# A two-layer decoder trunk: the mLSTM group's projections folded into score and gate weights, loras by differences, two longer pauses

## The chip, the core and the metric

The kernel runs on one core of a Trainium2 chip. The metric is the device time of one execution in microseconds (us). Each core has a matrix engine (TensorE, "PE" in the profile; its weight loads are "PEld"), a vector engine (VectorE, "DVE"), a scalar engine (ScalarE, "ACT"), a small general engine (GpSimd, "POOL"), and SyncE ("SP"), whose in-order queue issues all the DMA transfers of this kernel.

## The reference, cut to what matters

There are 256 tokens of 2048 features, in float32, and two layers. Layer 0 makes `u = h @ w_in`, and its columns feed two groups that run side by side. One is an RG-LRU. The other is an mLSTM group, which the change touches:

```python
xmc = silu(causal_dwconv(xm, m_conv_w, m_conv_b))
q = block_diag(xmc, m_wq)          # 512 blocks of 4x4
k = block_diag(xmc, m_wk)
v = block_diag(xm, m_wv)
qkv = concatenate([q, k, v])
ig = qkv @ m_wi + m_bi             # 8 heads
fg = qkv @ m_wf + m_bf
ym = mlstm_chunkwise(q, k, v, ig, fg)   # needs the scores q @ k^T
```

Layer 1 is RWKV-7 time mixing. Two low-rank branches ("loras") take shifted inputs:

```python
dh = shift_right(h) - h
xw = h + dh * mu_w;  xa = h + dh * mu_a
w_log = ... tanh(xw @ w1) @ w2 ...
a     = sigmoid(a0 + (xa @ a1) @ a2)
```

and the delta rule is computed in chunks of 64 tokens, for which triangular 64x64 matrices are inverted, 32x32 blocks first, which are then merged.

## The kernel before

All large products run on TensorE with each weight split in two parts (`whi`, made by ScalarE, and `wlo`, the rest, made by VectorE), and the activations likewise (`hh`, `hl`). A weight piece is 128x1024 (512 KB). `load_w` fetches it through SP's queue into one of four `raw` buffers, `split_w` makes the two parts (three buffers each), and `in_mms` issues the matmuls into the banks `gb`. An input projection (`in_proj`) takes 8 such pieces of 24 matmuls and gives 512 columns of `u`.

All work around these products is written as Python generators. Each runs in a lane of a small planner (`Weave`). A generator issues some instructions and then yields a number, its pause, in units of the planner's clock; `in_mms` moves that clock on by 0.44 after every few matmuls (`wv_.tick`), 2.64 per piece. When a pause is over, the next section of the generator is issued between the matmuls. `wv_.drain(gen)` runs a generator to its end at once. TensorE's order is exactly this order of issue (`InOrder`). The other engines' queues are ordered by a scheduler, in which the splits of the weights go ahead of other work; each queue is then executed in order.

The parts that the change touches:

- `mlstm_in(c, xm)`, for the quarters c = 0 to 3 of the mLSTM group (512 features, two heads each). It runs the convolution, forms `xm2` = 2 silu(conv), spreads the 4x4 blocks into block-diagonal 128x128 weights `we` (VectorE), multiplies (q and k on TensorE, copied to `qk`; v in token order, copied to `vtok`), sums up the gates' pre-activations (from `wif`, q, k, and `gv`, the v projection folded into the gate weights) and the scores `S`. The generator of quarter c is still under way when the next input projection ends, and is drained there, so its TensorE part lies in one block between two projections.
- `tables()` loads and prepares constants during the first projection; `gates()` turns the gates' sums into the row `Mt` per head; `head(hd)` spreads that row over 128 partitions by a matmul with `sel`.
- `loras()` in layer 1: 8 pieces of 128x384. Per piece VectorE makes `wb` from the loaded lora weights `raw` and the vectors mu (three products, three differences), then follows the split, and 18 matmuls. The three banks' parts `q0`, `q1`, `q2` give `hid`.
- `decay(g, st)` for the groups g = 0 to 7 of layer 1: it loads the second lora weight `l2` (named `l` in the profile) and multiplies it with `hid`. From its results come `Pe`, then `keys` makes `AR` and `BK`, and `blocks` needs these.
- `inverse(g, st)`: VectorE inverts the 32x32 blocks; two rounds of small matmuls then merge them. The first round is `mb<-ZT,Aab`; ScalarE copies the result into `ZT`; the second is `mb<-TT,ZT`. Between the two stands a pause (`yield 2.6`).

Most matmuls are issued at L117, and the instructions of VectorE and ScalarE at L133, the helpers' lines; groups are therefore told apart by their tiles.

Of the kernel before, what the change touches and what calls it, by code (L numbers as in the profile page):

```python
# [144 lines left out]
def two_layers(ctx, tc, x, gpost, cst, selc, v0, v1, w_in0, w_out0, w_in1, w_out1, lruw, qkvw,  # L145
# [274 lines left out]
    with ExitStack() as l0:  # L420
# [36 lines left out]
        wiff = c0.tile([P, 2048], F32, name="wif", tag="wg")[:, 0:1920].rearrange("p (a b) -> p a b", a=48)  # L457
        qkvs = c0.tile([P, 4, 16, 4], F32, name="qkvs")
        sel = c0.tile([8, 8, P], F32, name="sel")
# [40 lines left out]

        def mlstm_in(c, xm):
            xc = t4("xc")
            for f in range(4):
                i = 4 * c + f
                conv(xc[:, f, :], xm[:, f, :], [vs0(f"mw{j}", i) for j in range(4)], vs0("mb", i))
                yield 6.76
# [5 lines left out]
            we = [t4("we") for _ in range(2)]  # L512
            wv = [w.rearrange("p a t -> p (a t)").rearrange("p (w f o) -> p w f o", w=2, f=4) for w in we]
            for m in range(4):
                for f in range(4):
                    dve.tensor_tensor(
                        wv[m // 2][:, m % 2, f, :].rearrange("p (b o) -> p b o", o=4),
                        qkvs[:, m, 4 * c + f, :].unsqueeze(1).broadcast_to([P, 32, 4]),
                        blk.unsqueeze(2).broadcast_to([P, 32, 4]), MUL)
                yield 4.0 if m == 3 else 1.0  # L520
            wq, wk, wvv, wvT = (wv[m // 2][:, m % 2] for m in range(4))
            qk = [t4("qk") for _ in range(2)]
            for f in range(4):
                b = mbank()
                pe.matmul(b[:, 0:T], lhsT=wq[:, f, :], rhs=xm2[:, f, :], start=True, stop=True, skip_group_check=True)
                pe.matmul(b[:, T:2 * T], lhsT=wk[:, f, :], rhs=xm2[:, f, :], start=False, stop=True, skip_group_check=True)
                activ(qk[f // 2][:, 2 * (f % 2):2 * (f % 2) + 2, :], b.rearrange("p (a t) -> p a t", a=2), AF.Copy, scale=0.5)
                yield 0.6
            qt = lambda f: qk[f // 2][:, 2 * (f % 2), :]
            kt = lambda f: qk[f // 2][:, 2 * (f % 2) + 1, :]  # L530
# [7 lines left out]
            gv = s0.tile([P, 160], F32, name="gv", tag="gv", bufs=1)  # L538
            b = mbank()
            for f in range(4):  # L540
                pe.matmul(b[:, f * 40:(f + 1) * 40], lhsT=wvT[:, f, :], rhs=wiff[:, 32 + 4 * c + f, :],
                          start=(f == 0), stop=True, skip_group_check=True)
            dve.tensor_copy(gv, b[:, 0:160])
            yield 0.96

            ops = []
            for f in range(4):
                i = 4 * c + f
                ops += [(wiff[:, i, :], qt(f)), (wiff[:, 16 + i, :], kt(f)), (gv[:, f * 40:(f + 1) * 40], xm[:, f, :])]
            b = mbank()  # L550
            for n, (w, r) in enumerate(ops):
                o = b[64 * (n % 2):64 * (n % 2) + 40, 0:T]
                pe.matmul(o, lhsT=w, rhs=r, start=(n < 2), stop=(n >= 10), skip_group_check=True)
                if n % 4 == 3:
                    yield 0.5
# [6 lines left out]
            for hd in range(2):  # L562
                b = mbank()
                for j, (lo_, w_) in enumerate(((0, T), (P, P))):
                    o = b[:, 0:T] if j == 0 else b[:, T:T + P]
                    for f in range(2):
                        pe.matmul(o, lhsT=kt(2 * hd + f)[:, j * P:(j + 1) * P], rhs=qt(2 * hd + f)[:, lo_:T],
                                  start=(j == 0 and f == 0), stop=(f == 1), skip_group_check=True)
                activ(S[:, 2 * c + hd, :], b[:, 0:384], AF.Copy, scale=0.0625)
                yield 0.8  # L570

        gt = c0.tile([8, 8, T], F32, name="gt", tag="wg")
        gf, gi, e, r1, r2, r3, aj, Mt = (gt[:, i, :] for i in range(8))
# [168 lines left out]
    with ExitStack() as l1:  # L742
# [39 lines left out]
        def loras():  # L782

            banks = [gbank(), gbank()]
            for pc in range(8):
                raw = wp.tile([P, 2, 512], F32, name="raw", tag="raw", bufs=RAW_BUFS)
                nc.sync.dma_start(raw[:, :, 0:192], lora1[pc].rearrange("p (k f) -> p k f", k=2))
                wb = t4("wb", (2, 384))
                for wc, oc, n, nm in ((0, 128, 96, "muw"), (160, 224, 32, "mua"), (96, 320, 64, "mua")):
                    ac = {128: 0, 224: 96, 320: 256}[oc]  # L790
# [10 lines left out]
            act.copy(sh[0:64, 0, :], q2[64:128])
            act.copy(sh[64:96, 0, :], q1[96:128])
            dve.tensor_tensor(hid[:, 1, 1:T], hid[:, 1, 1:T], sh[:, 0, 0:T - 1], ADD)
            activ(hid[:, 0, :], hid[:, 0, :], AF.Tanh)
# [145 lines left out]
        def inverse(g, st):  # L950
# [47 lines left out]
            yield 2.6  # L998
# [313 lines left out]
```

## Time and profile before

| | |
|---|---|
| runs | 1907.44, 1913.1 and 1910.84 us, median 1910.84 |
| profiled execution | 1908.97 us, its span 1907.2 us, granted TensorE clock 0.993 |
| TensorE busy | 1877.9 us (98%) |
| VectorE, ScalarE, GpSimd busy | 1394.5 us (73%), 1057.2 us (55%), 63.3 us (3%) |
| DMA | 299.63 MB, 157 GB/s on average |

Layer 0's projections and heads lie in the first 470 us of the span, its output projection ends about 640 us, and layer 1 fills the rest. In the rows of the timeline the first number is the start in us from the span's start, the second how long the row's group lasts, then come engine, line, operation, output tile <- input tiles, rows*columns of the array that a matmul uses, its output's shape, and how many. "mb" and "gb" are banks of the results' memory. A float32 matmul of the program is two instructions in the trace; a split one is one. A time in square brackets is idle time of the engine before the row, and what ended it. Since matmuls are pipelined, the distance between two starts tells what one costs in a stream, not its own duration.

### The profile page before, as it was taken

Reading aid. Unit: us, or ns where it says so; the run is one execution under the profiler, and the core shown is the slowest. Engines: PE = TensorE matmul, PEld = TensorE weight load, DVE = VectorE, ACT = ScalarE, POOL = GpSimd, SP = SyncE. Lnnn points to the kernel's source line nnn. Section 1 sums busy time; section 2 is a strip of 40 time slices with the busy share of each in tenths; the row PEclk is TensorE's granted clock in tenths of the full one; section 3 lists DMA queues with packets and bytes.
Section 4 is the critical chain, followed back from the end, with each engine's and each line's share of the span. In section 5 each row is a group of like instructions: output and inputs, shape, how many; then the busy total and the mean of one; then the engine's idle time right before and its main releaser. Section 6 shows DMA issues by size and latency. Waiting matters only on the chain.

```text
span 1907.2 us, 39575 instructions
## 1 busy us (share of the span) xinstructions
PE 1877.9 (98%) x16507; PEld 1738.9 (91%) x16507; DVE 1394.5 (73%) x2302; ACT 1057.2 (55%) x1633; POOL 63.3 (3%) x92
## 2 busy tenths in 40 slices
PE   9999999999999999999999999999999999999998
PEld 8999999999888899989999999999999999997886
DVE  5667777766554669979689689597697896895544
ACT  5444666644444546565565656655655655665442
POOL 0000000000000000000010010000100100100000
PEclk9999999999999999999999999999999999999999
DMA  7433545445655543434434334344344333356654
GB/s 250 143 133 111 175 159 176 150 171 187 225 201 203 176 144 131 154 120 145 145 131 144 123 131 156 117 147 145 109 155 138 138 134 133 123 183 210 213 199 158
DMA packets 86947, 299.63 MB, mean 157 GB/s; under 512 B 9576, under 2 KB 12392, under 8 KB 86768
## 3 DMA queue, kind: packets, MB, share of 16 engines
q1 hardware_dynamic: 86768, 297.11, 45.0%
q8 instruction: 129, 2.11, 0.4%
q14 instruction: 50, 0.41, 0.1%
HBM read 289.20 MB, written 7.86 MB: 156 GB/s over the span
## 4 chain that ended last, share of the span: by engine, by line
PE 90%; DVE 5%; ACT 2%; issue 1%; DMA 1%; POOL 0%; DVEq 0%; SPq 0%; POOLq 0%; ACTq 0%
PE gb L117 73%; PE mb L117 16%; DVE wlo L133 2%; PE mb L120 2%; ACT whi L133 1%; DVE bi L133 1%; DVE wb L133 1%; ACT ZT L133 0%; ACT bh L133 0%; DMA raw<-in_w_in_dram 0%; DMA xq<-in_x_dram 0%; DVE rt L133 0%; DVE Tb L133 0%; DMA yraw<-y1d 0%; ACT vt L133 0%
## 5 line engine op out<-in xcount | busy, mean ns | idle before, releaser
L133 DVE TENSOR_TENSOR wlo<-raw,whi 128x1024 fp32r<-128x1024 f32 x509 | 619.7, 1219 | 333.7 <-ACT whi L133 299.4
L133 ACT CAST whi<-raw 128x1024 fp32r<-128x1024 f32 x509 | 532.3, 1048 | 511.1 <-PE gb L117 464.2
L117 PE MATMUL gb<-hh,whi 128*128 128x256 f32 x3120 | 794.3, 290 | 2.9 <-ACT whi L133 2.9
L117 PE MATMUL gb<-hl,whi 128*128 128x256 f32 x3120 | 773.6, 284 | 0.9 <-DVE hl L133 0.9
L117 PEld LDWEIGHTS gb<-hh,whi 128*128 128x128 f32 x3120 | 598.9, 192 | 13.7 <-ACT whi L133 3.7
L117 PEld LDWEIGHTS gb<-hl,whi 128*128 128x128 f32 x3120 | 599.8, 192 | 2.3 <-DVE hl L133 1.5
L117 PE MATMUL gb<-hh,wlo 128*128 128x256 f32 x3120 | 453.4, 286 | 0.0
L117 PEld LDWEIGHTS gb<-hh,wlo 128*128 128x128 f32 x3120 | 405.2, 191 | 4.3 <-issue 0.7
L117 PE MATMUL gb<-whi,yl 128*128 128x512 f32 x500 | 137.2, 392 | 0.5 <-DVE yl L133 0.5
L117 PE MATMUL gb<-whi,yh 128*128 128x512 f32 x500 | 136.2, 391 | 0.0
L117 PE MATMUL gb<-wlo,yh 128*128 128x512 f32 x500 | 135.7, 391 | 0.0
L117 PEld LDWEIGHTS gb<-whi,yl 128*128 128x128 f32 x500 | 93.0, 188 | 20.4 <-DVE yl L133 1.0
L117 PEld LDWEIGHTS gb<-wlo,yh 128*128 128x128 f32 x500 | 93.5, 188 | 19.7
L117 PEld LDWEIGHTS gb<-whi,yh 128*128 128x128 f32 x500 | 93.1, 188 | 19.4
L133 DVE TENSOR_TENSOR Tb<-Tb,tf 64x31 f32<-64x31 f32 (+15 forms) x248 | 82.5, 333 | 6.1
L133 DVE TENSOR_TENSOR tf<-Ab,Tb 64x31 f32<-64x31 f32 (+15 forms) x248 | 81.8, 330 | 4.5
L117 PE MATMUL mb<-AR,BK 64*128 64x128 f32 (+1 forms) x1024 | 58.0, 253 | 6.9 <-DVE AR L133 6.0
L117 PEld LDWEIGHTS mb<-AR,BK 64*128 64x128 f32 (+1 forms) x1024 | 50.2, 161 | 13.3 <-PE gb L117 7.0
L133 DVE TENSOR_TENSOR UV<-mb,Gn 64x256 f32<-64x256 f32 x64 | 26.9, 421 | 34.5 <-PE mb L117 33.4
L133 ACT ACTIVATE zz<-kP,dv 128x256 f32<-128x256 f32 x64 | 32.3, 505 | 23.5 <-DVE kP L133 12.4
L1150 POOL TENSOR_TENSOR vr<-vr,mhalf 128x8 f32<-128x8 f32 x16 | 28.3, 1770 | 490.7 <-DVE vr L133 490.7
L117 PEld LDWEIGHTS mb<-UV,At 128*64 128x64 f32 (+1 forms) x1024 | 35.0, 137 | 10.3 <-issue 2.5
(262 smaller groups left out, 1848.9 us busy)
## 6 DMA issues: line engine op xcount, KB each, us to landing
raw<-in_w_in_dram SPq DMA_DIRECT2D x384, 512.0 KB, 3.2
raw<-in_w_out_dram SPq DMA_DIRECT2D x128, 512.0 KB, 4.2
y1d<-zt SPq DMA_DIRECT2D x7, 512.0 KB, 3.5
yraw<-y1d SPq DMA_DIRECT2D x7, 512.0 KB, 4.1
l<-in_lora_dram SPq DMA_DIRECT2D x8, 384.0 KB, 4.3
xq<-in_x_dram SPq DMA_DIRECT2D x8, 256.0 KB, 5.3
lw<-in_lruw_dram SPq DMA_DIRECT2D x4, 512.0 KB, 4.9
xr<-in_x_dram SPq DMA_DIRECT2D x8, 256.0 KB, 6.2
```

Of the source, the lines that this page charges most:

```text
L117: return self._chain(self.eng.matmul(*a, **k))
L120: return self._chain(self.eng.transpose(**k))
L133: r = op(*a, **k)
L1150: pool.tensor_tensor(vr, vr, mhalf[:, 0:8], ALU.pow)
```

## The change

1. q and k are no longer formed. The scores are xm2^T (Wq Wk^T) xm2, and Wq Wk^T is again made of 4x4 blocks (`Xc`). One block-diagonal product per 128 features, `wx` (in `pp` after the copy), takes the place of two.
2. The gates' weights are folded likewise, once per quarter and on VectorE, at the quarter's beginning: `gate_weights(c)` multiplies the rows of `wif` with the 4x4 blocks and adds up, which gives `gw`, two sets of weights that act on `xm2` and on `xm` directly. For this every partition needs the four gate rows of its block. `gate_rows` loads them with 12 small transfers per quarter (80 KB each, runs of 640 bytes) into `wr`, for quarter 0 in `tables()`, for the next ones during the convolution of the quarter before. The weights `we` are also made at the beginning, ahead of the convolution.
3. `sel` and `Mt` (now in `Mr`) are padded with zeros from 8 to 128 partitions.
4. `loras()` splits the loaded weights and mu times the weights, without the differences; these are taken on the results, h W - h (mu W) + shift(h (mu W)), after the matmuls.
5. Pauses: in `decay` 6 in place of 4 for g = 0, in `inverse` 4.2 in place of 2.6. `l2` is loaded by three transfers in place of one.
6. `vec1` and the rest of `cs` are loaded in `gates()` and no longer at the beginning.

```diff
@@ tables()
-            nc.sync.dma_start(qkvs, qkvw)
+            nc.sync.dma_start(qkvs, qkvw[:, 0:3])
+            for i in range(4):
+                nc.sync.dma_start(krep[i:P:4].rearrange("p j t o -> p j (t o)"), rows(qkvw[:, 1].rearrange("p t o -> p (t o)")))
             nc.sync.dma_start(cs0, cst[:, NC1:NC])
-            nc.sync.dma_start(sel, selc)
+            nc.sync.dma_start(sel[0:8], selc)
...
-            nc.sync.dma_start(wiff, wif)
-            nc.sync.dma_start(vec1, v1)
-            nc.sync.dma_start(cs[:, 128:NC1], cst[:, 128:NC1])
+            dve.tensor_tensor(krep, krep, qkvs[:, 0].unsqueeze(1).broadcast_to([P, 4, 16, 4]), MUL)
+            dve.tensor_reduce(Xc, krep, mybir.AxisListType.X, ADD)
+            dve.tensor_scalar(qkvs[:, 0:2], qkvs[:, 0:2], 0.5, None, MUL)
+            for m in range(3):
+                gate_rows(0, m)
@@ new
+        def gate_rows(c, m):
+            if m == 0:
+                wrs[c] = c0.tile([P, 12, 160], F32, name="wr", tag="wg")
+            src = rows(wif[:, 16 * m + 4 * c:16 * m + 4 * c + 4].rearrange("p t n -> p (t n)"))
+            for i in range(4):
+                nc.sync.dma_start(wrs[c][i:P:4, 4 * m:4 * m + 4], src)
+
+        def gate_weights(c):
+            wr = wrs.pop(c)
+            gw = s0.tile([P, 2, 160], F32, name="gw", tag="gw", bufs=1)
+            for m in range(3):
+                w = qkvs[:, m, 4 * c:4 * c + 4, :].rearrange("p t o -> p o t")
+                r = wr[:, 4 * m:4 * m + 4].rearrange("p o (t n) -> p o t n", t=4)
+                dve.tensor_tensor(r, r, w.unsqueeze(3).broadcast_to([P, 4, 4, 40]), MUL)
+            for to, a, n in ((0, 0, 8), (1, 8, 4)):
+                while n > 2:
+                    n //= 2
+                    dve.tensor_tensor(wr[:, a:a + n], wr[:, a:a + n], wr[:, a + n:a + 2 * n], ADD)
+                dve.tensor_tensor(gw[:, to], wr[:, a], wr[:, a + 1], ADD)
+            return gw
@@ mlstm_in(c, xm)
+            (8 products for we, then gw = gate_weights(c))
             xc = t4("xc")
             for f in range(4):
                 conv(xc[:, f, :], ...)
+                if f and c < 3:
+                    gate_rows(c + 1, f - 1)
                 yield 6.76
...
-            (16 products for we: wq, wk, wvv, wvT)
-            for f in range(4):
-                b = mbank()
-                pe.matmul(b[:, 0:T], lhsT=wq[:, f, :], rhs=xm2[:, f, :], ...)
-                pe.matmul(b[:, T:2 * T], lhsT=wk[:, f, :], rhs=xm2[:, f, :], ...)
-                activ(qk[f // 2][...], b..., AF.Copy, scale=0.5)
+            for f2 in range(2):
+                b = mbank()
+                for f in range(2):
+                    pe.matmul(b[:, f * T:(f + 1) * T], lhsT=wx[:, 2 * f2 + f, :], rhs=xm2[:, 2 * f2 + f, :], ...)
+                act.copy(pp[:, 2 * f2:2 * f2 + 2, :], b...)
...
-            for f in range(4):
-                pe.matmul(b[:, f * 40:(f + 1) * 40], lhsT=wvT[:, f, :], rhs=wiff[:, 32 + 4 * c + f, :], ...)
-            dve.tensor_copy(gv, b[:, 0:160])
...
-                ops += [(wiff[:, i, :], qt(f)), (wiff[:, 16 + i, :], kt(f)), (gv[:, f * 40:(f + 1) * 40], xm[:, f, :])]
+                ops += [(gw[:, 0, f * 40:(f + 1) * 40], xm2[:, f, :]), (gw[:, 1, f * 40:(f + 1) * 40], xm[:, f, :])]
...
-                        pe.matmul(o, lhsT=kt(2 * hd + f)[:, j * P:(j + 1) * P], rhs=qt(2 * hd + f)[:, lo_:T], ...)
+                        pe.matmul(o, lhsT=xm2[:, 2 * hd + f, j * P:(j + 1) * P], rhs=pp[:, 2 * hd + f, lo_:T], ...)
@@ head(hd)
-            pe.matmul(b[:, 0:T], lhsT=sel[:, hd, :], rhs=Mt, start=True, stop=True, skip_group_check=True)
+            pe.matmul(b[:, 0:T], lhsT=sel[:, hd, :], rhs=Mr, start=True, stop=True, skip_group_check=True)
@@ loras()
-                    dve.tensor_tensor(wb[:, :, oc:oc + n], raw[:, :, wc:wc + n], mu, MUL)
-                    dve.tensor_tensor(wb[:, :, ac:ac + n], raw[:, :, wc:wc + n], wb[:, :, oc:oc + n], SUB)
-                in_mms(banks, *split_w(wb, 384), pc, h, 3, 0.0)
+                    dve.tensor_tensor(wb[:, :, oc:oc + n], raw[:, :, wc:wc + n], mu, MUL)     # wb = raw[:, :, 192:384]
+                in_mms(banks, *split_w(raw, 384), pc, h, 3, 0.0)
...
-            (5 copies, 2 additions, tanh)
+            (6 copies, 2 differences, 2 additions, tanh)
@@ decay(g, st)
-            yield 2.8 if g else 4
+            yield 2.8 if g else 6
-            nc.sync.dma_start(l2, lora2[:, g, :, :])
+            nc.sync.dma_start(l2[:, 0, :], lora2[:, g, 0, :])
+            nc.sync.dma_start(l2[0:64, 1, :], lora2[32:96, g, 1, :])
+            nc.sync.dma_start(l2[64:96, 1, :], lora2[0:32, g, 1, :])
@@ inverse(g, st)
-            yield 2.6
+            yield 4.2
```

The order in which the instructions stand, at three places. First TensorE, at the block of quarter 0 behind the second input projection. Before:

```order
L117 MATMUL gb<-hh,wlo 128x256 x8
L117 MATMUL mb<-xm_792,we 128x256 x8
L117 MATMUL mb<-we,xm 128x128 x8
L117 MATMUL mb<-wif,we 128x40 x4
L117 MATMUL mb<-qk,wif 40x256 x2
L117 MATMUL mb<-xm,gv 40x256
```

and with the change (`xm_844` is `xm2`):

```order
L117 MATMUL gb<-hh,wlo 128x256 x8
L117 MATMUL mb<-xm_844,we 128x256 x4
L117 MATMUL mb<-we,xm 128x128 x8
L117 MATMUL mb<-xm_844,gw 40x256
L117 MATMUL mb<-xm,gw 40x256
```

Four of the eight wide products and the four matmuls that made `gv` are gone, and the gates take eight matmuls in place of twelve; the block keeps its place behind the same projection.

Second TensorE again, at the merge of group 2 in layer 1, from a little ahead of its second round (the first round, `mb<-ZT,Aab`, stands 24 projection matmuls ahead of it before, 36 with the change). Before:

```order
L117 MATMUL mb<-TT,ZT 32x32 x32
L117 MATMUL gb<-hh,whi 128x256
L117 MATMUL gb<-hl,whi 128x256
L117 MATMUL gb<-hh,whi 128x256
L117 MATMUL gb<-hl,whi 128x256
L117 MATMUL mb<-centre,vt 128x128 x8
```

and with the change:

```order
L117 MATMUL mb<-centre,vt 128x128 x8
L117 MATMUL gb<-hh,whi 128x256
L117 MATMUL gb<-hl,whi 128x256
L117 MATMUL gb<-hh,whi 128x256
L117 MATMUL gb<-hl,whi 128x256
L117 MATMUL gb<-hh,wlo 128x256 x4
L117 MATMUL mb<-TT,ZT 32x32 x32
```

The second round now stands behind the products with `centre` (of `values`, which need `vt`); 28 projection matmuls lie between the first round and these.

Third VectorE, at the end of the keys of group 0, where its last `BK` is made. Before:

```order
L133 TENSOR_TENSOR BK<-xx,zz 128x4x64
L133 TENSOR_TENSOR AR<-rt,Pe 128x4x64
L133 SCALAR_TENSOR_TENSOR rt<-gb,vec_81,rt 128x255
L133 TENSOR_TENSOR BK<-xx,zz 128x4x64
L133 TENSOR_TENSOR AR<-rt,Pe 128x4x64 x2
L133 TENSOR_TENSOR Aab<-mb,Gn 64x2x256 x4
```

and with the change:

```order
L133 SCALAR_TENSOR_TENSOR rt<-gb,vec_81,rt 128x255
L133 TENSOR_TENSOR BK<-xx,zz 128x4x64
L133 TENSOR_TENSOR AR<-rt,Pe 128x4x64 x2
L133 TENSOR_TENSOR BK<-xx,zz 128x4x64
L133 TENSOR_TENSOR Aab<-mb,Gn 64x2x256 x2
L133 TENSOR_TENSOR BK<-xx,zz 128x4x64
L133 TENSOR_TENSOR Aab<-mb,Gn 64x2x256 x2
```

The last `BK` now stands behind two of the four `Aab`, which need results of TensorE. The matmuls `mb<-AR,BK` that need it keep their place among the projection's; the two groups `mb<-hid,l` that begin group 0's chain stand 20 and 16 projection matmuls later.

More of the change, by code (lines that the diff above doesn't have):

```diff
@@ L454, in two_layers @@
         h = to_features(xs, [scale(ss[tt], s0) for tt in range(2)], lambda i: vs0("pre", i), (0, 0))
-        wiff = c0.tile([P, 2048], F32, name="wif", tag="wg")[:, 0:1920].rearrange("p (a b) -> p a b", a=48)
-        qkvs = c0.tile([P, 4, 16, 4], F32, name="qkvs")
-        sel = c0.tile([8, 8, P], F32, name="sel")
+        qkvs = c0.tile([P, 3, 16, 4], F32, name="qkvs")
+        krep = c0.tile([P, 4, 16, 4], F32, name="krep")
+        Xc = c0.tile([P, 4, 16], F32, name="Xc")
+        rows = lambda w: w.rearrange("(b o) r -> b o r", o=4)
+        sel = c0.tile([P, 8, P], F32, name="sel")
+        Mr = c0.tile([P, T], F32, name="Mr")
+        pool.memset(sel, 0.0)
+        pool.memset(Mr, 0.0)
         gbs = c0.tile([8, 2], F32, name="gbs")
@@ L499, in two_layers @@
         xm2s = []
-        def mlstm_in(c, xm):
+        def gate_rows(c, m):
[17 more added lines that the diff above has]
+            return gw
+        wrs = {}
+        def mlstm_in(c, xm):
+            we = t4("we").rearrange("p a t -> p (a t)").rearrange("p (w f o) -> p w f o", w=2, f=4)
+            for m in range(2):
+                for f in range(4):
+                    i = 4 * c + f
+                    dve.tensor_tensor(
+                        we[:, m, f, :].rearrange("p (b o) -> p b o", o=4),
+                        (Xc[:, :, i] if m == 0 else qkvs[:, 2, i, :]).unsqueeze(1).broadcast_to([P, 32, 4]),
+                        blk.unsqueeze(2).broadcast_to([P, 32, 4]), MUL)
+            wx, wvv = we[:, 0], we[:, 1]
+            gw = gate_weights(c)
             xc = t4("xc")
@@ L511, in mlstm_in @@
             dve.scalar_tensor_tensor(xm2, th, 1.0, xc, ADD, MUL)
-            we = [t4("we") for _ in range(2)]
-            wv = [w.rearrange("p a t -> p (a t)").rearrange("p (w f o) -> p w f o", w=2, f=4) for w in we]
-            for m in range(4):
-                for f in range(4):
[L516 to L522, printed above, removed]
-            for f in range(4):
+            yield 4.6
+            pp = t4("pp")
+            for f2 in range(2):
                 b = mbank()
-                pe.matmul(b[:, 0:T], lhsT=wq[:, f, :], rhs=xm2[:, f, :], start=True, stop=True, skip_group_check=True)
-                pe.matmul(b[:, T:2 * T], lhsT=wk[:, f, :], rhs=xm2[:, f, :], start=False, stop=True, skip_group_check=True)
-                activ(qk[f // 2][:, 2 * (f % 2):2 * (f % 2) + 2, :], b.rearrange("p (a t) -> p a t", a=2), AF.Copy, scale=0.5)
+                for f in range(2):
+                    pe.matmul(b[:, f * T:(f + 1) * T], lhsT=wx[:, 2 * f2 + f, :], rhs=xm2[:, 2 * f2 + f, :],
+                              start=(f == 0), stop=True, skip_group_check=True)
+                act.copy(pp[:, 2 * f2:2 * f2 + 2, :], b.rearrange("p (a t) -> p a t", a=2))
                 yield 0.6
-            qt = lambda f: qk[f // 2][:, 2 * (f % 2), :]
-            kt = lambda f: qk[f // 2][:, 2 * (f % 2) + 1, :]
             for tt in range(2):
@@ L552, in mlstm_in @@
                 o = b[64 * (n % 2):64 * (n % 2) + 40, 0:T]
-                pe.matmul(o, lhsT=w, rhs=r, start=(n < 2), stop=(n >= 10), skip_group_check=True)
+                pe.matmul(o, lhsT=w, rhs=r, start=(n < 2), stop=(n >= 6), skip_group_check=True)
                 if n % 4 == 3:
@@ L797, in loras @@
             act.copy(hid[:, 0, :], q0[0:96])
-            dve.tensor_tensor(hid[:, 0, 1:T], hid[:, 0, 1:T], q1[0:96, 0:T - 1], ADD)
-            act.copy(hid[0:64, 1, :], q2[0:64])
+            act.copy(hid[0:64, 1, :], q1[0:64])
             act.copy(hid[64:96, 1, :], q0[96:128])
[L801 to L804, printed above, removed]
+            act.copy(sh[:, 1, :], q2[0:96])
+            act.copy(sh[0:64, 0, :], q1[64:128])
+            act.copy(sh[64:96, 0, :], q2[96:128])
+            for k in range(2):
+                dve.tensor_tensor(hid[:, k, :], hid[:, k, :], sh[:, 1 - k, :], SUB)
+                dve.tensor_tensor(hid[:, k, 1:T], hid[:, k, 1:T], sh[:, 1 - k, 0:T - 1], ADD)
+                if k == 0:
+                    activ(hid[:, 0, :], hid[:, 0, :], AF.Tanh)
         def shifted(banks, sec, g, o):
```

22 lines of the change are left out of this document (9 added, 13 removed).

## The prediction

> **What bounds the kernel now.** I read the page first, then the busy time by stretches, then the timeline of TensorE at the places that the change touches, with the other engines beside it.
>
> ```profile
> PE 1877.9 (98%) x16507; PEld 1738.9 (91%) x16507; DVE 1394.5 (73%) x2302; ACT 1057.2 (55%) x1633; POOL 63.3 (3%) x92
> PE 90%; DVE 5%; ACT 2%; issue 1%; DMA 1%; POOL 0%; DVEq 0%; SPq 0%; POOLq 0%; ACTq 0%
> 60.00:100.00 40.00, 40.00 (x318) 37.81 (x317) 25.65 (x56) 19.00 (x26) 0.00 (x0) 1.00 0.37 128
> ```
>
> TensorE is busy 98% of the span and carries 90% of the chain that ended last. In the stretch from 60 to 100 us, a quarter of the mLSTM group, it is busy all 40 us, VectorE 25.65, ScalarE 19.00, and the transfer engines 0.37 of the time. So matmuls taken out of that stage shorten the kernel, and VectorE work of some us put in costs nothing as long as it comes in time. Behind it, time is to be had only where TensorE waits: at the loras and at the merges.
>
> **Folded mLSTM, TensorE's part (A).** The block of one quarter:
>
> ```profile
> 99.56 3.62 PE L117 MATMUL mb<-xm,we 128*128 128x256 f32 x16
> 103.02 1.95 PE L117 MATMUL mb<-we,xm 128*128 128x128 f32 x16
> 104.80 0.98 PE L117 MATMUL mb<-wif,we 128*128 128x40 f32 x8
> 105.71 0.63 PE L117 MATMUL mb<-qk,wif 128*40 128x256 f32 x4
> ...
> 108.60 2.88 PE L117 MATMUL mb<-qk 128*128 128x256 f32 x16
> 111.24 0.36 PE L117 MATMUL gb<-hh,whi 128*128 128x256 f32 x1
> ```
>
> From start to start: the 16 instructions for q and k take 103.02 - 99.56 = 3.46 us, 0.216 each; half go, 1.73. The product for `gv` (104.80 to 105.71), 0.91, goes. The gates take 108.60 - 105.71 = 2.89 for 12 matmuls that run in pairs; four go, 0.96. That is 3.60 per quarter and 14.4 for four; I keep back 0.05 per quarter for the step to 40 columns, which stays, and take 14.2. Nothing in the block waits for a projection matmul, so this is time of the path. The most is 14.4; 13.0 if each block gains a short wait of 0.35 (the scores now need the copies `pp`, but the products with `we` and the gates, some 3.5 us, lie between).
>
> **Its VectorE part.** The rows of the same stage (66 to 101 us):
>
> ```profile
> L133 DVE TENSOR_TENSOR wlo<-raw,whi 128x1024 fp32r<-128x1024 f32 x9 | 11.0, 1224 | 10.2 <-ACT whi L133 10.1
> L133 DVE TENSOR_TENSOR we<-qkvs,cs 128x128 f32<-128x128 f32 x16 | 3.6, 285 | 0.0
> ```
>
> Eight of the 16 `we` go: -1.8 us. `gate_weights` adds three products and one sum of 640 columns, two sums of 320 and two of 160. Between the 0.285 us of 128 columns and the 1.224 of 1024 these are, by estimate, 0.8, 0.5 and 0.3 us, 4.8 together. So 3 us more per quarter lie in the 14 us that VectorE had free of 40; ScalarE copies two banks fewer. I cost that at nothing: the new work stands at the quarter's beginning, a whole projection (192 matmuls of 0.12, 23 us) ahead of its use. If the cover failed, TensorE would wait for `gw` in the block, up to 3 us each.
>
> **`sel` on 128 rows (B).** Two rows around one head's matmul, two around a full one:
>
> ```profile
> 216.76 0.28 PE L117 MATMUL gb<-hl,whi 128*128 128x256 f32 x1
> 216.97 0.69 PE L117 MATMUL mb<-gt,sel 8*128 8x256 f32 x2
> 217.81 0.28 PE L117 MATMUL gb<-hl,whi 128*128 128x256 f32 x1
> 187.86 0.28 PE L117 MATMUL gb<-hl,whi 128*128 128x256 f32 x1
> 187.98 1.03 PE L117 MATMUL mb<-yc,lw 128*128 128x256 f32 x4
> 188.97 0.28 PE L117 MATMUL gb<-hl,whi 128*128 128x256 f32 x1
> ```
>
> With 8 rows, two instructions and two projection matmuls take 217.81 - 216.76 = 1.05 us; with 128 rows, four and two take 1.11, so two and two would take 1.11 - 2 x 0.216 = 0.68. That is 0.37 for each of 8 heads: 3.0 us, all on the path. Bounds 0 (if the excess belongs to the step from projection to small matmul and stays) and 3.0. [...]
>
> **The beginning (C).** In SP's queue four `krep` loads come ahead of the second piece of weights, and the load before it (`gbs`) has to wait for the landing of the first.
>
> ```profile
> 6.84 6.32 DMA raw<-in_w_in_dram
> 17.07 1.04 ACT L133 CAST whi<-raw 128x1024 fp32r<-128x1024 f32 x1
> raw<-in_w_in_dram SPq DMA_DIRECT2D x384, 512.0 KB, 3.2
> ```
>
> The first piece lands at 13.16; the second is then issued at about 13.5 and lands, at 3.2 us, at 16.7, where ScalarE splits it at 17.07 today. Three more crowd behind it. I take 0.5 us lost, between 0 and 3.2 (a whole landing that nothing covers).
>
> **Loras (D).**
>
> ```profile
> 685.75 0.49 DVE L133 TENSOR_TENSOR wb<-raw,vec 128x192 f32<-128x192 f32 x2
> 686.15 0.49 DVE L133 TENSOR_TENSOR wb<-raw,wb 128x192 f32<-128x192 f32 x2
> 686.55 0.28 DVE L133 TENSOR_TENSOR wb<-raw,vec 128x128 f32<-128x128 f32 x1
> 686.87 0.29 DVE L133 TENSOR_TENSOR wb<-raw,wb 128x128 f32<-128x128 f32 x1
> 687.28 0.83 ACT L133 CAST whi<-wb 128x768 fp32r<-128x768 f32 x1 [2.44 <-DVE wb L133]
> 689.02 0.49 DVE L133 TENSOR_TENSOR wb<-raw,vec 128x192 f32<-128x192 f32 x2
> 679.04 0.28 PE L117 MATMUL gb<-hh,whi 128*128 128x256 f32 x1
> 691.43 0.38 PE L117 MATMUL gb<-hh,whi 128*128 128x256 f32 x1 [0.85 <-ACT whi L133]
> 700.22 0.28 PE L117 MATMUL gb<-hh,whi 128*128 128x256 f32 x1
> ```
>
> VectorE and ScalarE need 689.02 - 685.75 = 3.27 us per piece, one after the other; TensorE's 18 matmuls need 18 x 0.12 = 2.16 (0.12 is the step from 187.86 to 187.98 above). TensorE lives on its lead and then waits: the eight pieces last 700.22 - 679.04 = 21.18 us, where the matmuls are 17.28. Without the differences (0.40 at 686.15, 0.32 at 686.87) the period is 2.55, and the last piece, ready at 697.9 today, is ready 5.8 us sooner, 2 us before TensorE wants it. So all 3.9 us come back; 2.5 if the longer hold on `raw` (until `wlo` is made) delays a load.
>
> **The later second lora (E).** `hid` takes a copy, two differences and an addition more, and the pause is longer.
>
> ```profile
> 710.57 1.89 PE L117 MATMUL mb<-hid,l 96*128 96x256 f32 x8
> 735.53 0.68 PE L117 MATMUL mb<-AR,BK 64*64 64x64 f32 x14 [0.81 <-DVE BK L133]
> ```
>
> The second group of `mb<-hid,l` stands 16 matmuls later, 1.9 us. The whole chain from there to `BK` hangs on it, and at 735.53 TensorE waits for `BK` already. `mb<-AR,BK` keeps its place, so this wait grows by 1.9, and by up to 1.3 more since the last `BK` stands behind two `Aab` in VectorE's queue (512 columns each; an estimate from the 1.224 us of 1024). I take 2.4 lost, between 0.5 (the splits of weights in between come earlier too) and 3.5. The shorter loras thus pay for less than they free. A longer pause before `mb<-hid,l` frees nothing of its own: the profile shows no wait there.
>
> **The merge (F).**
>
> ```profile
> PE mb L117 <- ACT ZT L133: 5.8, 11, 0.8
> 1051.11 1.20 PE L117 MATMUL mb<-ZT,Aab 32*32 32x32 f32 x64
> 1055.09 0.28 PE L117 MATMUL gb<-hl,whi 128*128 128x256 f32 x1
> 1056.09 0.24 PE L117 MATMUL mb<-TT,ZT 32*32 32x32 f32 x2 [0.72 <-ACT ZT L133]
> 1056.69 1.19 PE L117 MATMUL mb<-TT,ZT 32*32 32x32 f32 x62 [0.36 <-ACT ZT L133]
> 1055.51 0.87 DVE L133 SCALAR_TENSOR_TENSOR vt<-gb,vec,vt 128x255 f32<-128x255 f32 x2
> ```
>
> The waits' row counts 5.8 us in 11 waits, two in each of groups 2 to 6 and one in group 7. From start to start one merge loses 1056.69 - 1055.09 = 1.60, less some 0.22 for the matmul and the step to small ones: 1.38, five times, and 0.6 in group 7: 7.5 us. With the change the second round comes 12 matmuls and the products with `centre` later (1.44 us, and 1.78 as the 16 alike from 103.02 to 104.80), behind 1056.69, so this wait ends. Next late is `vt`: the `centre` products would begin at 1055.7, and their last features need the `vt` that VectorE ends at 1056.38, where TensorE would be at 1056.1 to 1056.3. I count 0.35 back in five groups: F = 7.5 - 1.7 = 5.8, between 3.0 and 7.5. What comes behind (`UV`, `Ws`) keeps its places.
>
> **The rest.** Three loads in place of one for `l2` cost SP two issues more per group, and the loads of `vec1` are only later: nothing, since SP mostly waits for buffers (row below).
>
> **Sum.** 14.2 + 3.0 - 0.5 + 3.9 - 2.4 + 5.8 = 24.0 us. The profiled execution took 1908.97 us (1.8 around its span), which gives 1885.0. It lies 1.9 under the median of the runs, from which it would be 1886.9; I say 1886. What a measurement can tell from no change here is 0.3%, 5.7 us.
>
> **Rivals.**
>
> Slower: the small transfers. Twelve stand in SP's queue ahead of weight loads of the next quarter.
>
> ```profile
> SPq L218 <- DVE wlo L133: 113.6, 32, 14.1
> raw<-in_lora_dram SPq DMA_DIRECT2D x8, 192.0 KB, 2.7
> ```
>
> In the first 180 us SP waits 113.6 us for raw buffers, 3.55 per weight load, 28 per quarter of 8 loads. If a small transfer took the queue the whole 2.7 us to landing, as nearest row the loras' 768-byte runs, twelve would take 32, of which 4 us per quarter come through: 16 in all, 1901. To be slower by 5.7 us the four sets must cost 24.0 + 5.7 = 29.7, 7.4 each, which is so from (28 + 7.4)/12 = 2.95 us a transfer on; 3.5 us would give (42 - 28) x 4 = 56 lost, 1941. Against it: those landings overlapped, eight loads being in flight at once, so one should hold the queue for 2.7 / 8 = 0.34 us, by estimate, and twelve for 4 of the 28. [...]
>
> The merge's wait only moves, to `centre` or to `Ws` behind the later `TT`: F is 0, 1892. For it speaks `vt`'s end at 1056.38.
>
> The folded block waits inside, for `gw` or `pp`, and keeps half of A: 1893.
>
> Group 0 loses all that the loras gain and more (E is -6): 1890.
>
> `sel`'s rows don't matter (B is 0): 1889.
>
> The change does nothing in sum, several covers failing at once: 1909.
>
> **Chances.** The sum as worked out 0.52; the merge's wait moves 0.13; half of A 0.12; group 0 0.08; `sel` 0.08; transfers, slower 0.03, or no change 0.04. All but the last two are faster by over 0.3%: 0.93; within 0.3% 0.04; slower 0.03. The range: all upper ends give 14.4 + 3.0 + 0 + 3.9 - 0.5 + 7.5 = 28.3, 1880.7, and a run 3 us under the median 1878. Upward it takes in the rivals at 1889 to 1893 and a part of two of them together: 1897.
>
> **What would show it.** In the profile after: TensorE's block of a quarter lasts 8.1 us in place of 11.7, with no wait in brackets; `mb<-Mr,sel` in pairs of 0.22; loras 17.3 us long without a wait for `whi`; the wait for `BK` in group 0 about 3 us in place of 0.81; no wait for `ZT`, perhaps short ones for `vt`. Wrong it would be by waits of TensorE for `whi` in the first 180 us (transfers), or for `gw`.

## The result, and the profile after

The changed kernel takes 1886.34 us (median of four runs, 1884.82 to 1889.29), the kernel before 1911.13 (four runs, 1907.44 to 1913.1): a ratio of 0.9874, 95% interval 0.9855 to 0.9894. The prediction was 1886. The profiled execution after took 1884.82 us, its span 1883.0, at a mean granted clock of 0.996 (0.993 before). Two runs of the kernel before that stand beside the experiments took 2245 and 2561 us at a clock of 0.75 and 0.65; they are left out of the ratios and averages.

The page's line of busy times and the line of the chain that ended last:

```profile
PE 1856.2 (99%) x16410; PEld 1723.5 (92%) x16411; DVE 1400.9 (74%) x2279; ACT 1052.2 (56%) x1626; POOL 63.4 (3%) x94
PE 92%; DVE 5%; issue 1%; ACT 1%; DMA 1%; POOL 0%; SPq 0%; DVEq 0%; POOLq 0%; ACTq 0%
```

The stretch from 60 to 100 us (busy time and count of PE, PEld, DVE, ACT, POOL, then granted clock, DMA share, GB/s):

```profile
60.00:100.00 40.00, 40.00 (x317) 38.22 (x316) 30.87 (x51) 21.34 (x31) 0.00 (x0) 1.00 0.55 185
```

TensorE still has no gap in the mLSTM stage, although VectorE is busy for 30.87 us there in place of 25.65. The timeline of TensorE shows the block of quarter 1 and one head:

```profile
96.43 1.89 PE L117 MATMUL mb<-xm,we 128*128 128x256 f32 x8
98.16 1.95 PE L117 MATMUL mb<-we,xm 128*128 128x128 f32 x16
100.04 1.93 PE L117 MATMUL mb<-xm,gw 128*40 128x256 f32 x16
101.89 2.88 PE L117 MATMUL mb<-pp,xm 128*128 128x256 f32 x16
104.53 0.36 PE L117 MATMUL gb<-hh,whi 128*128 128x256 f32 x1
...
203.03 0.28 PE L117 MATMUL gb<-hl,whi 128*128 128x256 f32 x1
203.15 0.60 PE L117 MATMUL mb<-Mr,sel 128*128 128x256 f32 x2
203.40 0.47 PE L117 MATMUL gb<-hh,whi 128*128 128x256 f32 x1
203.71 0.28 PE L117 MATMUL gb<-hl,whi 128*128 128x256 f32 x1
```

The block lasts 104.53 - 96.43 = 8.10 us, no row has a wait in brackets, and two and two at a head take 203.71 - 203.03 = 0.68. These are the rows of TensorE's waits that moved (before: ZT 5.8 in 11 waits, whi 2.9 in 4, BK 0.8, yl 0.5, none for At):

```profile
PE mb L117 <- DVE BK L133: 2.9, 4, 1.4
PE mb L117 <- DVE At L133: 2.6, 2, 2.2
PE gb L117 <- DVE yl L133: 2.0, 2, 1.5
PE gb L117 <- ACT whi L133: 0.6, 1, 0.6
PE mb L117 <- ACT ZT L133: 0.3, 1, 0.3
```

The projection's 9360 matmuls are the same in both traces and all recorded, so the start of the n-th before, less its start after, tells what has been gained up to there. That difference, stage by stage:

| stage | term | predicted | gained in the trace |
|---|---|---|---|
| start, first two weight pieces | C | -0.5 | -0.4 |
| four mLSTM blocks (3.46 to 3.58 each) | A | +14.2 | +14.1 |
| eight heads (0.39 each) | B | +3.0 | +3.1 |
| loras | D | +3.9 | +3.9 |
| group 0, second lora to the products with BK | E | -2.4 | -5.5 |
| rest of groups 0 and 1 | | 0 | -3.6 |
| merges of groups 2 to 6 | F | +5.2 | +13.8 |
| last group, out projection's begin | F | +0.6 | -1.2 |
| sum | | 24.0 | 24.2 |

(F's 5.8 is 1.38 - 0.35 in each of five groups and 0.6 in the last.) The sum is right and the last four rows are not. The 13.8 are not even: groups 3 and 5 give 1.15 each, groups 2, 4 and 6 give 3.84. Here are stretches of the kernel before, around group 2's merge and 34 us later (columns as above):

```profile
1055.37:1058.78 3.41, 2.34 (x72) 2.19 (x73) 3.23 (x7) 3.15 (x6) 0.00 (x0) 1.00 0.61 214
1058.78:1062.20 3.42, 3.42 (x18) 3.42 (x18) 0.18 (x1) 2.24 (x7) 0.00 (x0) 0.50 0.45 153
1089.51:1092.92 3.41, 3.41 (x41) 3.21 (x40) 2.77 (x6) 2.09 (x6) 0.00 (x0) 1.00 0.27 92
1092.92:1096.33 3.41, 3.41 (x28) 3.07 (x28) 2.68 (x7) 1.89 (x3) 0.00 (x0) 0.50 0.16 61
```

After the merge's waits (TensorE busy 2.34 of 3.41 us) the granted clock is 0.50 for 3.41 us, which is called a stretch at half clock from here on. Group 2's products with `centre` stand there:

```profile
1058.39 3.25 PE L117 MATMUL mb<-centre,vt 128*128 128x128 f32 x16
1061.30 0.56 PE L117 MATMUL gb<-hh,whi 128*128 128x256 f32 x1
```

and in the kernel after:

```profile
1044.02 2.21 PE L117 MATMUL mb<-centre,vt 128*128 128x128 f32 x16
1045.98 0.36 PE L117 MATMUL gb<-hh,whi 128*128 128x256 f32 x1
```

2.91 us against 1.96 for the same 16 instructions. Before has six such stretches between 1058 and 1622 us, in groups 2, 4 and 6, whose begins lie whole multiples of 3.413 us apart (1058.78 to 1092.92 is 10.0 of them), which is called the trace's grid from here on; after has none behind a merge, but four ahead of group 2's merge (two in a row from 716.20 on, 876.62, 948.30). The experiments ask what these stretches cost and where the losses in groups 0 and 1 come from.

### The profile page after: what moved, and what is told of

It reads as the page before. It is cut to its first block, busy times and chain, and to the rows that moved or that the text cites. A ratio compares the mean times of both kernels' runs of the same rounds, so it can differ in the third digit from the quotient of the medians.

```text
span 1883.0 us, 39445 instructions
## 1 busy us (share of the span) xinstructions
PE 1856.2 (99%) x16410; PEld 1723.5 (92%) x16411; DVE 1400.9 (74%) x2279; ACT 1052.2 (56%) x1626; POOL 63.4 (3%) x94
## 4 chain that ended last, share of the span: by engine, by line
PE 92%; DVE 5%; issue 1%; ACT 1%; DMA 1%; POOL 0%; SPq 0%; DVEq 0%; POOLq 0%; ACTq 0%
PE gb L117 75%; PE mb L117 15%; DVE wlo L133 2%; PE mb L120 2%; DVE Tb L133 0%; DVE tf L133 0%; DMA raw<-in_w_in_dram 0%; DVE yT L133 0%; DVE rt L133 0%; ACT whi L133 0%; DMA xq<-in_x_dram 0%; DVE hl L133 0%; POOL vr L1186 0%; DVE AR L133 0%; DVE Ab L133 0%
## 5 line engine op out<-in xcount | busy, mean ns | idle before, releaser
L133 DVE TENSOR_TENSOR wlo<-raw,whi 128x1024 fp32r<-128x1024 f32 (+1 forms) x517 | 627.2, 1214 | 316.7 <-ACT whi L133 278.6
L133 ACT CAST whi<-raw 128x1024 fp32r<-128x1024 f32 (+1 forms) x517 | 538.5, 1044 | 519.5 <-PE gb L117 454.6
L117 PE MATMUL mb<-UV,At 128*64 128x64 f32 (+1 forms) x1024 | 43.8, 228 | 0.0
```

Source lines behind the costliest of these rows:

```text
L117: return self._chain(self.eng.matmul(*a, **k))
L133: r = op(*a, **k)
```

## The experiments

Each ran beside the kernel before on the same chip (medians 1910.55 to 1911.17 there). The changed kernel was not run again beside them, so a difference from its median is one between sessions. Lines are those of the kernel named first. "Aligned" means that starts of the same projection matmuls are compared, as for the table above.

**The merge's pause alone.**

```diff
 before, inverse()
-            yield 2.6
+            yield 4.2
```

> The kernel before with one edit, the pause of the merge 4.2 in place of 2.6. What is to be told apart: what the merge term F is made of. In the traces of before and after, aligned by the projection's matmuls, one merge gives 1.16 us in groups 3 and 5, but 3.84 in groups 2, 4 and 6; there the clock record of before shows a stretch of 3.41 us at half clock behind the merge (1058.78, 1321.61, 1584.44), and another some 34 us later (1092.92, 1355.74, 1618.57). Theory 1 (waits alone, as predicted): 5 x 1.16 = 5.8 us gained, less some 2.4 for the wait for At that group 1 shows after the change (its scores stand later with the longer pause): about 1907.5. Theory 2 (a wait of about 1 us among small matmuls also sets the clock to half for the next 3.41 us): the three stretches behind merges go too, 1.6 each; about 1903, less if the stretches 34 us later go as well (1900). Either way no wait for ZT in groups 2 to 6, and in the clock record none behind a merge by theory 2.

1900.71 us, ratio 0.9949 (0.9936 to 0.9962): 9.8 gained. No wait for `ZT`, and no stretch behind a merge: theory 2. In the aligned starts groups 2 to 6 give 11.7, though two stretches of its own, each 34 us behind a merge, take 2.2 of it. Groups 0 and 1 lose 3.7: TensorE waits 2.04 us (start to start) for `At` at 891.04, half clock from 891.34 on, as it does after, and 2.0 us for `yl` at the end. So these losses belong to the merge's pause, which also moves the scores of group 1 by 16 matmuls.

**Useless matmuls in the wait.**

```diff
 before, inverse()
             tb = [mbank(), mbank()]
+            for _ in range(9 if 1 < g < 7 else 0):
+                pe.matmul(tb[0][:, 0:T], lhsT=bonesr, rhs=h[0][0][:, 0, :], start=True, stop=True, ...)
```

> The kernel before, its pauses unchanged, with nine matmuls of 128x256 that nobody uses put right ahead of the merge's second round in groups 2 to 6 (9 x 0.12 = 1.08 us, as long as TensorE's two waits there, 0.72 + 0.36). They stand where TensorE idles, so no work is saved and none is moved. Theory 1 (the wait is all that the merge costs): no change, 1911. Theory 2 (the idle time among small matmuls takes the clock to half for the next 3.41 us): the stretches at half clock behind the merges go, three in the profiled execution, 1.6 us each: about 1906, and the products with centre take 1.96 us in every group in place of 2.91 in groups 2, 4, 6.

1903.09 us, ratio 0.9964 (0.9952 to 0.9976): 7.5 us faster by 45 matmuls that nobody uses. The timeline of TensorE in group 2:

```profile
1058.07 1.18 PE L117 MATMUL mb<-hh,bones 128*128 128x256 f32 x9
1059.18 1.56 PE L117 MATMUL mb<-TT,ZT 32*32 32x32 f32 x64
...
1061.26 1.95 PE L117 MATMUL mb<-centre,vt 128*128 128x128 f32 x16
```

and its row of waits for `ZT`:

```profile
PE mb L117 <- ACT ZT L133: 0.7, 3, 0.4
```

The filling ends where `ZT` comes, and `centre` runs at full clock. Aligned with before, groups 3 and 5 gain nothing (the filling costs what the wait did), groups 2, 4 and 6 gain 1.6 at the merge and 1.1 some 34 us later. So a merge's wait of 1.16 us cost 2.75 in groups 2, 4 and 6. This trace also has half clock where the order is still that of before and before ran at full clock, for 6.83 us from 822.90 on and 3.41 from 962.85 on, which cost it 4.0: where the stretches fell differed between these two executions.

**The loras alone.**

```diff
 before, loras() and the three loads of l2 as after; in decay()
             yield 2.8 if g else 4
```

> The kernel before with the new loras (and the three loads of l2 that they need), the pause ahead of the second lora as before, 4. It tells D and E apart. Theory (the pause costs and isn't needed): loras of 17.3 us, 3.9 gained, the second lora where it was, the wait for BK about 1 us as before or less: 1907. Rival (the pause pays: with 4, TensorE waits for hid or for l, whose load is issued in a queue and takes 6.7 us to land in the trace of after): a wait for l or hid of 1 to 2.5 us at the second lora of group 0, which passes on to BK: 1908 to 1910.

1910.8 us, ratio 0.9999 (0.9989 to 1.0008): nothing gained. The 3.9 us come back in the loras and are lost again at the second lora:

```profile
705.28 3.19 PE L117 MATMUL mb<-hid,l 96*128 96x256 f32 x8 [2.47 <-DMA l<-in_lora_dram]
```

and the stretches of 3.41 us around that wait:

```profile
702.61:706.03 3.42, 0.95 (x5) 0.56 (x4) 1.29 (x2) 0.07 (x1) 0.00 (x0) 1.00 1.05 278
706.03:709.44 3.41, 3.41 (x12) 2.89 (x12) 0.00 (x0) 1.68 (x4) 0.00 (x0) 0.50 0.51 203
```

The rival holds: the load of `l` is the next to be late, and a stretch at half clock follows its wait.

**The fold alone.** The changed kernel with the old loras, decay and merge and `sel` on 8 rows.

> The fold alone: the changed kernel with sel and Mt on 8 rows, the old loras, the old pauses. Theory: four blocks of 8.1 us in place of 11.7, 14.1 gained, 0.4 lost at the start: 1897.4. Rival (part of the gain after comes from moved work behind it, or is lost when the rest isn't there): anything but 13 to 14.5 us less. [...]

1899.72 us, ratio 0.9946 (0.9934 to 0.9957), 10.8 gained, outside the theory's 13 to 14.5. Up to the loras the aligned starts give 13.5, as worked out; behind, the profiled execution loses 5 again with hardly a wait more: half clock for nine times 3.41 us in place of six, two of them from 810 us on, where before ran at full clock. One kernel's runs differ in the same way: of the 47 runs of the kernel before beside the experiments, the six at a mean clock of 0.995 average 1908.0 us, the eleven at 0.991 average 1912.6. The five runs of the fold alone all lie at 0.991 to 0.993; whether by chance is not shown.

**`sel` on 8 rows again.**

```diff
 after, head()
-            pe.matmul(b[:, 0:T], lhsT=sel[:, hd, :], rhs=Mr, ...)
+            pe.matmul(b[:, 0:T], lhsT=sel[0:8, hd, :], rhs=Mt, ...)
```

> The changed kernel with the head's matmul on 8 rows again (sel and Mt), the rest as changed: term B alone undone. Theory (a float32 matmul over 8 rows costs more than one over 128 in this stream; after against before gave 0.39 us a head): 8 x 0.39 = 3.1 us more, 1889.5, and in the timeline the two projection matmuls and the two with sel last 1.05 us again. Rival (rows of the array don't matter): no change, 1886.3.

1892.07 us, ratio 0.9902 (0.9887 to 0.9917), 5.7 over the changed kernel's median. The aligned starts lose 0.39 at each head, 3.1 in all; the rest goes with the clock (0.992 to 0.995 in its runs, 0.993 to 0.996 in the changed kernel's). The same place as above shows:

```profile
203.34 0.28 PE L117 MATMUL gb<-hl,whi 128*128 128x256 f32 x1
203.54 0.69 PE L117 MATMUL mb<-Mr,sel 8*128 8x256 f32 x2
204.17 0.39 PE L117 MATMUL gb<-hh,whi 128*128 128x256 f32 x1
204.39 0.28 PE L117 MATMUL gb<-hl,whi 128*128 128x256 f32 x1
```

1.05 us again where 128 rows take 0.68.

**Gate rows in 48 transfers.**

```diff
 after, gate_rows()
-                nc.sync.dma_start(wrs[c][i:P:4, 4 * m:4 * m + 4], src)
+                for j in range(4):
+                    nc.sync.dma_start(wrs[c][i:P:4, 4 * m + j:4 * m + j + 1], src[:, j:j + 1])
```

> The changed kernel with each of the 12 gate transfers of a quarter cut into four of 20 KB: 48 per quarter in SP's queue ahead of the same weight loads, the bytes unchanged. Theory (a small transfer holds the queue only while it is issued, 0.4 to 0.6 us as the three loads of l show after the change; SP has 28 us of waiting per quarter): 48 x 0.5 = 24 us, still covered, 1886 to 1888 and no wait for whi in quarters 1 to 3; the twelve for quarter 0 are 48 in the first 60 us and may cost a few us there, up to 1895. Rival (a transfer holds the queue until it lands, 2.4 us): 115 us per quarter, some 80 us of waits for whi in each of three quarters, above 2100.

1948.81 us, ratio 1.0200 (1.0185 to 1.0215): neither. SP's queue in quarter 0 of the kernel after:

```profile
47.57 8.24 SPq L517 DMA_DIRECT2D wr<-in_wif_dram  x12
```

and in this one, the set for quarter 0, the set for quarter 1, and TensorE's wait for weights behind each:

```profile
15.30 31.69 SPq L518 DMA_DIRECT2D wr<-in_wif_dram  x48
52.22 0.58 PE L117 MATMUL gb<-hh,whi 128*128 128x256 f32 x1 [18.64 <-ACT whi L133]
...
68.29 31.82 SPq L518 DMA_DIRECT2D wr<-in_wif_dram  x48
104.68 0.58 PE L117 MATMUL gb<-hh,whi 128*128 128x256 f32 x1 [10.34 <-ACT whi L133]
```

and its row of waits:

```profile
PE gb L117 <- ACT whi L133: 52.9, 5, 18.6
```

A transfer holds the queue for 0.69 and 0.66 us, not until it lands (2.4 after, 2.1 here). But 48 in a row keep the weights away for 31.7 and 31.8 us, and the buffers' lead doesn't last that long. The waits make up 52.9 of the 62.5 us over the changed kernel's median; half clock behind the four long ones costs 1.3 to 2.1 each in the aligned starts. The waiting of SP summed over a quarter, which my theory compared it with, is not what covers a block of issues: what covers it is how far the loads are ahead at that moment.

**Groups 0 and 1 mended.**

```diff
 after
                 loras()            # ahead of it: load_l2(0, l20)
-            yield 2.8 if g else 6
+            yield 2.8 if g else 4
-            yield 4.2
+            yield 4.2 if g > 1 else 2.6
```

> The changed kernel with group 0's second lora weight loaded ahead of the loras, the pause ahead of the second lora 4 again, and the merge's longer pause only from group 2 on. It takes away what the change lost in groups 0 and 1. Theory: the second lora stands 16 to 20 matmuls sooner without a wait for l, the waits for BK (3.7 us with the steps, two stretches at half clock) shrink to about 1 us, the wait for At in group 1 (2.4 us and one stretch) goes, since its scores stand where they stood before; the wait for sq at 824 us of before (0.96 us, up to two stretches) comes back: some 5 to 8 us gained, 1880. Rival (the losses belong to the shorter loras: hid or BK is late wherever the second lora stands): no more than 2 us gained.

1880.94 us, ratio 0.9846 (0.9831 to 0.9860), 5.4 under the changed kernel's median. No wait for `l`, one for `BK` (0.81) in place of four, none for `At`; the wait for `sq` in group 1 is back, with 6.83 us at half clock. That is the theory's 1880, and the rival's 2 us are passed.

**Two more pauses.**

```diff
 the mended kernel, scores() and keys()
-            yield 2
+            yield 3.3 if g > 1 else 2
-            yield 2.4
+            yield 3.6 if g == 1 else 2.4
```

> As the kernel of the groups 0 and 1, and besides the pause ahead of the scores' first product 3.3 in place of 2 from group 2 on (TensorE waits there for AR, 1.15 us in each of six groups), and the keys' pause 3.6 in place of 2.4 in group 1 (the wait for sq). Theory 1 (waits alone): 6 x 1.15 + 0.96 = 7.9 us less than that kernel, 1872. Theory 2 (with the clock): the stretches at half clock behind those waits go as well, 1.1 to 1.7 us each, 1 to 4 of them: 1866 to 1870. Rival (the wait only moves to the next product or to what needs the scores): under 2 us less.

1889.06 us, ratio 0.9881 (0.9865 to 0.9898), 8.1 slower than the mended kernel. The waits for `AR` are gone, and from group 2 on each group gains 1.76 at the first product and loses 2.16 at the later ones (waits for `At`, 2.9 us in 8, and blocks of 1.4 to 1.6 us in place of 1.1 to 1.2): the wait only moved, as the rival has it. In group 1 a wait of 2.3 us for `UV` and its half clock cost some 7.

**The 128x2 blocks in halves.** The stretch of before at 1092.92 follows 3.41 us in which TensorE was busy all the time (by the profile, which models the ends of matmuls), but 1.7 of them went to 16 matmuls of two columns (`mb<-cs,sq`).

```diff
 keys(), in the mended kernel and in before
-            yield 2.4
+            yield 1.6 if g else 2.4
                 ...
+                if f == 1 and g:
+                    yield 1.4
```

> The kernel of the groups 0 and 1 with one edit: from group 1 on the 16 matmuls of 128x2 (mb<-cs,sq), which stand in one block of 1.7 us, are issued in two halves, the first a little sooner, with 8 to 12 projection matmuls between. No work is saved. In the kernel before, the stretches at half clock 34 us behind a merge follow a window in which TensorE waits for nothing, but this block lies whole in it (1089.42 to 1091.13 in the window 1089.51 to 1092.92); in the kernel of groups 0 and 1 so do 803.37 (with a wait for sq of 0.98 us) and 1458.73. [...] Rival (only idle time of TensorE counts): the wait for sq goes, about 1 us, and 1458.73 or another behind such a block stays: 1880.

> The same edit in the kernel before. Theory (streaming counts): the stretches behind the blocks mb<-cs,sq go (three in the profiled execution, 1.1 us each, besides the wait for sq in group 1, 0.96 us), those behind the merges stay, since there the waits for ZT are unchanged: about 4 us less, 1906.5. Rival (idle time counts): 1 us less, 1910.

1889.79 us (ratio 0.9892, 0.9877 to 0.9908) and 1912.48 (1.0011, 1.0002 to 1.0020): 8.9 slower than the mended kernel and 1.3 slower than before, where all that was expected had said faster. In both no stretch lies behind such a block in groups 2 to 7 any more. But the edit also moved VectorE's work: `UV` in group 1 (2.0 us), `ZT` in group 1 (2.1) and `AR` in six groups (1.5 in place of 1.0) are now late, and in the second kernel the merges, whose waits shrank, lost their stretches too. Whether streaming or idle time counts is not shown by these two.

**The short pause in the changed kernel.**

```diff
 after, decay()
-            yield 2.8 if g else 6
+            yield 2.8 if g else 4
```

> The changed kernel with the pause ahead of group 0's second lora 4 again (the load of l where the change has it). Theory (the loras-only kernel: l lands too late for it): TensorE waits about 2.5 us for l at the second lora, with up to one stretch at half clock, and in turn about 1 us for BK in place of 3.7 with two stretches: within 2 us of the changed kernel, 1884 to 1888. Rival (the longer pause costs, as term E has it): no wait for l, 2.5 us or more gained, 1882 or less.

1881.63 us, ratio 0.9847 (0.9834 to 0.9861), 4.7 under the changed kernel. TensorE waits at the second lora and less at `BK`:

```profile
687.55 2.30 PE L117 MATMUL mb<-hid,l 96*128 96x256 f32 x8 [1.87 <-DMA raw<-in_w_in_dram]
...
717.04 0.67 PE L117 MATMUL mb<-AR,BK 64*64 64x64 f32 x14 [0.81 <-DVE BK L133]
```

(The three loads of `l` were issued from 680.6 to 681.6 and took 6.6 to 6.9 us, which is about when the wait ends; the row names another load that landed then.) Aligned with the changed kernel, 4.0 us are lost at the second lora, the 16 matmuls that stand earlier among them, and 7.0 come back at `BK`. Both stories were half right: the wait for `l` is there, and the longer pause still costs more than it saves.

**Useless matmuls once more.** Eight of them ahead of group 1's `mb<-cs,sq` in the mended kernel.

> The kernel of the groups 0 and 1 (second lora weight loaded early, short pause, longer merge pause from group 2 on) with eight matmuls of 128x256 that nobody uses put right ahead of the block mb<-cs,sq of group 1, where TensorE waits 0.98 us for sq and the clock record then shows 6.83 us at half clock (803.37). The order is otherwise the same. [...] Rival (the stretch comes from the block of 128x2 itself, which a filling ahead of it doesn't change): no change, 1881.

1880.08 us, ratio 0.9841 (0.9827 to 0.9854), the fastest median, though 0.9 under the mended kernel is within what the runs can tell. In the profile the wait for `sq` is filled, and 3.41 us at half clock follow in place of 6.83; the aligned starts gain 1.5 there.

## Why the prediction was right, point by point

The sum holds. Two of its terms do not, and that it holds all the same is luck, as the end of this section shows.

**A, B, C, D** came out as worked out: blocks of 8.10 us without a wait, pairs of 0.68 at the heads, 0.4 lost at the start (a wait for `whi` at 19.26), loras of 679.45 - 662.17 = 17.28 us. All four rest on distances between starts in the same stream. The rival by which `sel`'s rows don't matter is out: 8 rows cost 0.37 to 0.39 us more per head than 128 in this stream, and undoing B alone shows it again (1.05 us against 0.68).

**VectorE's cover and the transfers.** `gw` and `pp` are never waited for by TensorE. The work of `gate_weights` was put at 4.8 us a quarter and takes 4.9 (four instructions of 0.82, two of 0.48, two of 0.32). The estimate of 0.34 us per small transfer was half of the measured 0.69: it rested on eight loads in flight at once, but there are four `raw` buffers, and in before SP issues those eight over 23.76 us. Twelve hold the queue for 8.24 us, which the lead of the loads covers. The slower rival was right in kind: at 48 in a row it decides, through the time of issuing and not of landing.

**E was mis-sized**: -5.5 measured, -2.4 predicted, the lower bound -3.5. The wait for `BK` came as long as foreseen ("about 3 us"): four waits, 2.9 us, or 3.7 from start to start in place of 0.98:

```profile
714.08 0.33 PE L117 MATMUL mb<-AR,BK 64*64 64x64 f32 x2 [0.44 <-DVE BK L133]
715.22 0.67 PE L117 MATMUL mb<-AR,BK 64*64 64x64 f32 x14 [0.81 <-DVE BK L133]
716.22 0.47 PE L117 MATMUL mb<-AR,BK 64*64 64x64 f32 x2 [0.33 <-DVE BK L133]
718.05 1.11 PE L117 MATMUL mb<-AR,BK 64*64 64x64 f32 x14 [1.36 <-DVE BK L133]
```

and two stretches at half clock (716.20 to 723.03) cost the other half. The step that failed is the price of a wait: I counted its length alone. The rival for group 0 (E is -6), given a chance of 0.08, is nearer to the measured -5.5 than the sum is; its 1890 didn't come because F gave more. That the longer pause frees nothing was the right reading of its worth in the changed kernel (4.7 us faster without), though not for the reason given: with short loras there is a wait behind it, for `l`.

**F was mis-sized the other way**: +13.8 against +5.2 in groups 2 to 6. The waits themselves gave 1.15 to 1.16 per merge, 5.8 in five, where 1.38 had been counted less 0.35 for `vt`; no wait for `vt` or in `Ws` took their place, and the rival by which the wait only moves is out. The 0.6 of the last group did not show: `ZT` is no longer waited for there, but `yl` is. The other 8.0 were half clock: three stretches behind merges (1.6 each) and three 34 us later (1.1 each). The first three are shown to hang on the waits, by filling these. The later three lie behind the blocks `mb<-cs,sq` of the next group, which every kernel has: the profiled execution after shows one such (948.30), the mended one one besides group 1's (1458.73). The clock records of before and after tell which are hit. Of their twelve blocks in groups 2 to 7, four begin between 0.08 us before and 0.12 us after a point of the trace's grid (1089.42, 1352.36 and 1615.28 in before, 944.93 in after), and all four are followed by half clock; none of the other eight is, which begin 0.36 us before such a point or 0.41 us and more after one. So up to 3.3 of the 13.8 come from how these two executions fell on the grid, and not from the change itself.

**Not foreseen**: with the longer merge pause group 1's scores (`mb<-AR,BK`) stand 16 matmuls later; the instruction `At` that reads them then stands behind steps of the inversion in VectorE's queue, TensorE waits for it (2.24 us), and half clock follows. With the stretch at 948.30 (1.1) that makes -3.6 in groups 0 and 1. I had followed the pause in group 2 and not in the first two. At the end TensorE waits 2.0 us for `yl` in place of 0.5, as it does with the merge's pause alone.

So 24.2 against 24.0 is right by errors that nearly cancel (+8.6 for F in groups 2 to 6; -3.1, -3.6 and -1.8 against it). The largest part is of one kind: no term of the prediction had the clock in it, although the trace of before showed it.

## What to carry to other kernels

Price a wait of TensorE among small matmuls at more than its length (here 1.16 us cost 2.75 in groups 2, 4 and 6): read the granted clock of the few us behind it, and if it is 0.5, count that too. Where such a wait can't be removed, matmuls that nobody uses can be cheaper than idle time (here 45 of them made the kernel before 7.5 us faster). Align two traces by an instruction that is the same in both before believing a sum: terms of opposite sign hide in it. Read the clock records of both traces too, since a part of a difference between two executions can be the grid alone (here up to 3.3 of 24.2 us). And follow a changed pause through every round of its loop, the first ones above all.

## What the runs showed of the hardware

In the clock records of before and after TensorE's granted clock is 1.0 or 0.5. A stretch at half clock lasts 3.413 us there, or twice that (6.827 from 716.20 on in after), apart from one at the end of each (from 1901.88 and 1880.14 on), which runs on past the last instruction. Within one trace the begins lie whole multiples of 3.413 us apart: 1058.78 to 1321.61 is 77.0 of them in before, 716.20 to 876.62 is 47.0 in after. In before 1.07 to 1.11 us of waiting among the 64 matmuls of 32x32 of a merge's second round are followed by half clock in groups 2, 4 and 6, and not in 3 and 5. The three that are hit begin 0.71, 0.82 and 0.92 us after a point of the grid, the other two 0.39 and 0.49. In the filled kernel group 2's begins at 0.76, and no half clock follows. In before the next merge comes 130.1 us after one that is not hit, 38.13 times 3.413 us, and 132.8 after one that is, 38.90 times: the begin moves 0.4 us later on the grid until it is hit and 0.3 back then, which fits that every second merge of this trace is hit.

Half clock also follows 3.41 us in which TensorE is busy throughout, by the profile's modelled ends; here is one case, of the mended kernel:

```profile
1455.32:1458.73 3.41, 3.41 (x41) 3.21 (x40) 2.44 (x6) 2.42 (x7) 0.00 (x0) 1.00 0.11 43
1458.73:1462.14 3.41, 3.41 (x28) 3.19 (x27) 2.70 (x6) 1.30 (x2) 0.00 (x0) 0.50 0.28 111
```

What sets the clock to half behind such a stretch is not shown. Counted from the span's start, the grid's first point lies at 0.65 us in the trace of before and at 2.81 in that of after, so the two traces fall differently on it. The runs' spread (1907.2 to 1913.8 us for the kernel before, beside the experiments) goes along with their mean clock: 1908.0 us on average at 0.995, 1912.6 at 0.991.
